# Splitting all 41 weight pieces of the second block on GpSimd during the last feed-forward stage

## The chip, the core and the metric

The kernel runs on one core of a Trainium2 chip. The metric is device time in microseconds (us) of one launch. The median of three runs of the kernel before is 1818.0 us (1817.51 to 1821.33). All array data is float32; one core computes the whole program.

## The reference

Two blocks work on x, 512 tokens of 1024 features. The first block has two layers; each adds a mixer, a cross-attention and a feed-forward part, with a layer norm after each. The second block modulates the normalised result by a condition vector, projects it, and runs two kinds of attention on it:

```python
def conv_ffn(x, w_up, conv_w, conv_b, w_down):
    up = x @ w_up
    a, g = up[..., :D_FF], up[..., D_FF:]
    g = causal_dwconv(g, conv_w) + conv_b
    return (jax.nn.gelu(g) * a) @ w_down
...
        mod = c_act @ w_ada[l] + b_ada[l]
        shift, scale, gate = jnp.split(mod, 3, axis=-1)
        h = rms_norm(x, norm_g[l]) * (1.0 + scale[:, None, :]) + shift[:, None, :]
        proj = h @ w_in[l]
...
        y = jnp.concatenate([y_r * jax.nn.silu(g_r), y_a * jax.nn.silu(g_a)], axis=-1)
        x = x + gate[:, None, :] * (y @ w_out[l])
```

## The kernel before, in words

**Matmuls.** Activations lie transposed: 8 tiles of 128 features x 512 tokens. A product is made to nearly full float32 precision out of three float32r matmuls (`mm3`, lines 304 to 306): each operand is kept as a rounded part (hi) and a remainder (lo), and hi*hi, hi*lo and lo*hi are summed in PSUM. A weight *piece* is 128 x 1024, so 24 matmuls of 512 columns use one piece. Its hi and lo together are 1 MB, its raw form 512 KB.

**How a piece gets into SBUF.** `piece` loads the raw 512 KB on the SP queue (line 241) into a raw buffer (two `raw`, one `rawx`), ScalarE casts hi (line 229) and VectorE subtracts to get lo (line 230), both into a `w` or `wx` tile (4 + 2 in the first block). In the second block (`extra` is 0) the subtraction is GpSimd's, there are only the 4 `w` tiles, and both come under the same lines 229 and 230.

**Splitting ahead.** In the second layer's feed-forward stage `ffn(1, ...)` GpSimd, otherwise nearly idle, prepares pieces of the second block: `pre_step` copies one element of a fresh result into the load buffer (line 264; this only makes the load wait for that result, which paces it), loads the raw piece on its own queue (line 265), casts and subtracts (lines 271 and 272), and stores the 1 MB result in DRAM (line 275). Load and result share one of two `vt` tiles. One load is issued per call, and the split of the piece before it. There are 22 calls after hidden tiles and 16 after the first two down-projection chunks, for 28 pieces. `ready` later loads the 1 MB straight into a `w` tile on SP (line 282); pieces that are not prepared go through `piece`. Not prepared are the five `OPEN` pieces with which the second block begins (`open2`) and the eight pieces of the output projection (`out_begin`, `out_end`).

**The stages that matter here.** (1) At the end of the first cross-attention, `lin` runs its last six output pieces in token halves, and `ln_half` normalises the first half while TensorE works on the second: sums by `res_stat` on GpSimd (lines 411 and 412), an averaging matmul (line 429), then VectorE and GpSimd (lines 435 to 442). In the same stretch the vector `mod` is begun: `ada_step` loads `w_ada` in 48 parts of 256 KB into `kt` tiles on SP (line 722) and accumulates them on VectorE (lines 726 and 728). They belong to the next stage, but the scheduler, which fixes every queue's order when the program is built and draws a ready instruction forward into what it takes for a gap, has put them here. (2) The last feed-forward stage, about 1043 to 1409 us. (3) The seam: the norm of each half, then `modulate` (ScalarE squares at line 449, averaging matmuls at line 757, VectorE and ScalarE at lines 765 to 767), while TensorE works on the other half and on the five `OPEN` pieces. (4) The second block, whose chains of small VectorE steps are interleaved with weight matmuls by a hand-written list with costs (`ORDER`, `FILL`). (5) The end: outputs are gated (lines 1161 to 1169), four output pieces are begun with six of eight input tiles each, then `out_end` finishes these and does the other four.

Of the kernel before, what the change touches and what calls it, by code (L numbers as in the profile page):

```python
# [8 lines left out]
F32 = mybir.dt.float32  # L9
F32R = mybir.dt.float32r  # L10
# [29 lines left out]
FILL = (1.12, 3, 1.5, 4, 2.08, 4.16, 23.8, 9, 4.2, 0.4, 4)  # L40
DVE_SUB = (0, 2, 5)
OPEN = (16, 0, 4, 8, 1)
STAG = 0
LASTD = 6
KS = (0, 1, 2, 3, 4, 5)
NPART = 4
# [13 lines left out]
def f32(ap):  # L60
    return ap.bitcast(F32)
# [73 lines left out]
def layout(i):  # L135
    i = {k: np.asarray(v) for k, v in i.items()}
    a = {}
    a["cst"] = constants()
    a["vec"] = pack_vecs(i)
    a["xT"] = np.ascontiguousarray(i["x"][0].T).reshape(KT, P, S)  # L140
    a["memT"] = np.ascontiguousarray(i["mem"][0].T.reshape(4, 2, P, MEM).transpose(0, 2, 1, 3))
    w = i["ab_w_in"][0]
    a["ab_u"] = stationary(w[:, :512])
    a["ab_v"] = moving(w[:, 512:1024])
    a["ab_x"] = stationary(w[:, 1024:])
    a["ab_o"] = stationary(i["ab_w_out"][0])
    a["sgu_row"] = np.ascontiguousarray(
        np.concatenate([i["sgu_ln_g"][0], i["sgu_ln_b"][0], i["sgu_b"][0].reshape(-1)])[None])
    a["sgu_wT"] = np.ascontiguousarray(i["sgu_w"][0].transpose(2, 0, 1))
    a["pool_w"] = np.ascontiguousarray(i["pool_w"][0].transpose(1, 0, 2).reshape(P, 512))  # L150
    a["c_in"] = stationary(i["c_w_in"][0])
    a["c_o"] = stationary(i["c_w_out"][0])
    for l in range(2):
        a[f"xq{l}"] = stationary(i["xa_wq"][l])
        a[f"xk{l}"] = stationary(i["xa_wkv"][l][:, :D])
        a[f"xv{l}"] = moving(i["xa_wkv"][l][:, D:])
        a[f"xo{l}"] = stationary(i["xa_wo"][l])
        a[f"up{l}"] = stationary(i["ffn_w_up"][l])
        for c, (f0, f1) in enumerate(CHUNKS):
            a[f"dn{l}{c}"] = stationary(i["ffn_w_down"][l], f0 * P, f1 * P)  # L160
    a["ada"] = np.ascontiguousarray(i["w_ada_2"][0].reshape(KT, P, 6, S).transpose(0, 2, 1, 3))
    w = i["w_in_2"][0]
    a["in_r"] = stationary(w[:, :2688 + 512])
    a["in_va"] = moving(w[:, 3200:3712])
    a["in_ga"] = stationary(w[:, 3712:])
    a["lora"] = np.ascontiguousarray(np.concatenate([i["w2_2"][0], i["a2_2"][0]]))
    idx = np.clip(np.arange(64)[:, None] - np.arange(S)[None] + 448, -63, 128) + 63
    a["rb"] = np.ascontiguousarray(i["rel_bias_2"][0][:, idx]).reshape(4, P, S)
    a["out"] = stationary(i["w_out_2"][0])
    return a  # L170


class Prog:
# [69 lines left out]


    def pre_begin(self):
        self.prep, todo = {}, []
        for _, ws in ORDER:
            for w in ws.split("+"):
                k, m = w[0], int(w[1:])
                if k in "rq" and m not in OPEN:  # L250
                    todo.append(("in_r", m))
                elif k == "g":
                    todo.append(("in_r", 12 + m) if m < 4 else ("in_ga", m - 4))
                elif w == "v0":
                    todo += [("in_va", i) for i in range(4)]
        self.todo, self.due2 = todo, []

    def pre_step(self, at):

        nc = self.nc  # L260
        if self.todo:
            key = self.todo.pop(0)
            t = self.t("vt", [P, 2, D], F32, 2)
            nc.gpsimd.tensor_copy(t[:, 1, 0:1], at[:, 0:1])
            nc.gpsimd.dma_start(out=t[:, 1, :], in_=self.a[key[0]][key[1]])
            self.due2.append((key, t))
        if len(self.due2) > 1 or not self.todo:
            for key, t in self.due2[:1]:
                self.due2.pop(0)
                hi, lo = t[:, 0, :].bitcast(F32R), t[:, 1, :].bitcast(F32R)  # L270
                nc.gpsimd.tensor_copy(hi, t[:, 1, :])
                nc.gpsimd.tensor_tensor(out=lo, in0=t[:, 1, :], in1=t[:, 0, :], op=ALU.subtract)
                name = f"sp_{key[0]}{key[1]}"
                d = self.prep[key] = self.dram.tile([P, 2, D], F32, tag=name, name=name)
                nc.gpsimd.dma_start(out=d, in_=t)

    def ready(self, src, m):

        if (src, m) not in self.prep:
            return self.piece(self.a[src][m])  # L280
        w = self.wtile()
        self.nc.sync.dma_start(out=f32(w), in_=self.prep[src, m])
        return w
# [139 lines left out]
    def ln_half(self, ts):  # L423
# [14 lines left out]
        for k in range(KT):  # L438
            x = self.x[k][:, ts]
            gk, bk = self.v(g, layer * 8 + k), self.v(b, layer * 8 + k)  # L440
            (nc.vector if k in DVE_SUB else nc.gpsimd).tensor_tensor(out=x, in0=x, in1=mn, op=ALU.subtract)  # L441
            nc.vector.scalar_tensor_tensor(out=x, in0=x, scalar=gk, in1=rs, op0=ALU.mult, op1=ALU.mult)  # L442
            if split:
                hi, lo = self.xs[k][:, 0, ts], self.xs[k][:, 1, ts]
                nc.scalar.activation(hi, x, AF.Identity, bias=bk)  # L445
                nc.vector.scalar_tensor_tensor(out=lo, in0=x, scalar=bk, in1=f32(hi), op0=ALU.add, op1=ALU.subtract)  # L446
            else:
                self.sqs.append(self.t("kt", [P, S], F32, 8))
                nc.scalar.activation(self.sqs[k][:, :256], x, AF.Square, bias=bk)
        if split:  # L450
            for k in range(KT):
# [114 lines left out]
    def kv(self, l, tag):  # L566
        nc = self.nc
        mem = []
        for j in range(4):
            raw = self.t("kt", [P, S], F32, 8)  # L570
            nc.sync.dma_start(out=raw.rearrange("p (a b) -> p a b", a=2), in_=self.a["memT"][j])
            t = self.xh() if tag == "xh" else self.hd()
            self.split(t, raw)
# [8 lines left out]
        kt, vt = [], []  # L582

        def epi_k(m, ps, ts):
            t = self.t("kt", [P, 2, MEM], F32R, 8)
            kt.append(self.split(t, ps[:, :MEM]))

        self.lin(f"xk{l}", range(8), mem, epi_k, MEM)
        vt = [self.t("vt", [P, 2, D], F32R, 2) for _ in range(2)]
# [70 lines left out]
    def ffn(self, l, xs):  # L660
# [3 lines left out]
        for c, (f0, f1) in enumerate(CHUNKS):  # L664
# [3 lines left out]
            def epi(m, ps, ts):  # L668
# [9 lines left out]
                else:  # L678
# [1 line left out]
                    nc.vector.tensor_tensor(out=h, in0=ps, in1=keep["g"], op=ALU.mult)  # L680
                    hs.append(self.split(self.hd(), h))
                    if l == 1:
                        self.pre_step(f32(hs[-1][:, 0, :]))

            self.lin(f"up{l}", [o + f for f in range(f0, f1) for o in (NF, 0)], xs, epi, first=FIRST if c == 0 else 0)

# [3 lines left out]
            def epi_d(m, ps, ts):  # L690
# [5 lines left out]
                if c == 1 and l == 0 and m == 1:  # L696
                    self.ada_end()
                if c < 2 and l == 1:
                    self.pre_step(x)
                if c == 2:  # L700
                    self.res_stat(m, ts)

# [13 lines left out]

    def ada_step(self, f):
        nc = self.nc
        while self.ada_at < min(48, 3 * (f + 1)):
            k, part = divmod(self.ada_at, 6)  # L720
            raw = self.t("kt", [P, S], F32, 8)
            nc.sync.dma_start(out=raw, in_=self.a["ada"][k, part])
            dst = self.acc[part // 4][:, part % 4 * S : part % 4 * S + S]
            sc = self.cact[:, k : k + 1]
            if k == 0:
                nc.vector.tensor_scalar(out=dst, in0=raw, scalar1=sc, scalar2=None, op0=ALU.mult)
# [43 lines left out]
    def open2(self):  # L770
# [1 line left out]
        self.nw = 3  # L772
        self.due = []
        for i, m in enumerate(OPEN):
            self.due.append((m, self.piece(self.a["in_r"][m]), self.bank()))
            self.half2(*self.due[-1], HALVES[0])
            if i == DEFER:
                self.flush()
# [319 lines left out]
    def rwkv_chain(self, prs, tt):  # L1098
# [77 lines left out]
        n = 0  # L1176
        while any(lines):
            for i, g in enumerate(lines):
                if g and n >= i * STAG:
                    us = next(g, None)  # L1180
                    if us is None:
                        lines[i] = None
# [247 lines left out]
```

## Time and profile before

| | us |
|---|---|
| median of 3 runs | 1818.0 |
| the profiled execution | 1816.8 |
| its span, first to last instruction | 1815.0 |
| TensorE busy | 1765.0 |
| VectorE busy | 1085.1 |
| ScalarE busy | 745.6 |
| GpSimd busy | 429.9 |
| mean granted TensorE clock | 0.989 of full |

The rows name engines by PE (TensorE), DVE (VectorE), ACT (ScalarE), POOL (GpSimd), SP (SyncE, which only issues transfers). Times in a timeline are us from the span's start. A row of a timeline ends, in brackets, with the idle time of the engine before it and what ended that. "x4" after a row means four instructions in one piece.

### The profile page before, as it was taken

To read this page: it belongs to the slowest core of one execution; us is meant where nothing else is said; L and a number is where in the kernel's file an instruction comes from. 1 tells how busy PE (TensorE), PEld (TensorE's weight loads), DVE (VectorE), ACT (ScalarE), POOL (GpSimd) and SP (SyncE) were. 2 spreads that over 40 slices of the span, in tenths; PEclk is the share of its full clock that TensorE was granted. 3 is DMA by queue.
4 is the path that set the end of the run, shared out by engine and by line. 5 is a ranking of instruction groups with operands and counts; after the bars stand their busy time and mean duration, and the time that the engine had idled before them with its cause. 6 is when DMAs were issued, how large, how long until landed. Compare 5 with 4: busy or idle time off the path is not lost.

```text
span 1815.0 us, 26295 instructions
## 1 busy us (share of the span) xinstructions
PE 1765.0 (97%) x10452; PEld 1489.2 (82%) x10452; DVE 1085.1 (60%) x1679; ACT 745.6 (41%) x1237; POOL 429.9 (24%) x438
## 2 busy tenths in 40 slices
PE   8999998999999999999999999999999989999999
PEld 7889988888888898988998998888888866776667
DVE  5676689743453458544476585365354875773672
ACT  5544533532332346322265453133233653434561
POOL 0215015000000042000320524464455232210122
PEclk9999999999999999999999999999999999998999
DMA  8431355332323224433131146677663444461332
GB/s 279 157 103 56 129 179 184 119 102 93 93 81 107 85 64 145 150 101 99 53 114 50 47 163 243 221 256 264 210 236 124 126 167 173 164 208 70 130 125 95
DMA packets 70555, 252.54 MB, mean 139 GB/s; under 512 B 8224, under 2 KB 10912, under 8 KB 62752
## 3 DMA queue, kind: packets, MB, share of 16 engines
q1 hardware_dynamic: 54288, 188.51, 31.6%
q0 software_dynamic: 11312, 53.48, 8.6%
q10 hardware_dynamic: 4832, 8.88, 1.5%
q8 instruction: 82, 1.34, 0.3%
q14 instruction: 41, 0.34, 0.1%
HBM read 212.30 MB, written 38.54 MB: 138 GB/s over the span
## 4 chain that ended last, share of the span: by engine, by line
PE 79%; DVE 12%; ACT 4%; DMA 3%; issue 2%; POOL 0%; SPq 0%; ACTq 0%; DVEq 0%; POOLq 0%
PE ch L304 10%; PE ch L305 10%; PE ch L306 10%; PE mm L304 9%; PE mm L306 9%; PE mm L305 9%; PE pv L305 3%; PE pv L304 3%; PE pv L306 3%; PE ch L881 3%; DVE w L230 1%; DVE x L442 1%; DVE xh L446 1%; DVE x L441 1%; PE at L1240 1%
## 5 line engine op out<-in xcount | busy, mean ns | idle before, releaser
L304 PE MATMUL mm<-xh,w 128*128 128x512 f32 (+1 forms) x696 | 260.7, 375 | 8.5 <-ACT w L229 5.6
L306 PE MATMUL mm<-xh,w 128*128 128x512 f32 (+1 forms) x696 | 254.9, 366 | 0.8 <-DVE w L230 0.8
L305 PE MATMUL mm<-xh,w 128*128 128x512 f32 (+1 forms) x696 | 253.9, 365 | 0.0
L411 POOL TENSOR_TENSOR t<-x,x 128x512 f32<-128x512 f32 x6 | 8.9, 1480 | 690.7 <-DVE x L420 354.9
L304 PEld LDWEIGHTS mm<-xh,w 128*128 128x128 f32 x696 | 132.9, 191 | 35.0 <-issue 9.2
L229 ACT CAST w<-raw 128x1024 fp32r<-128x1024 f32 (+2 forms) x98 | 98.7, 1008 | 139.9 <-PE ch L306 62.2
L304 PE MATMUL ch<-xh,w 128*128 128x512 f32 (+1 forms) x432 | 152.4, 353 | 1.9 <-ACT xh L445 1.9
L305 PE MATMUL ch<-xh,w 128*128 128x512 f32 (+1 forms) x432 | 153.1, 354 | 0.8 <-DVE xh L446 0.5
L306 PEld LDWEIGHTS mm<-xh,w 128*128 128x128 f32 x696 | 133.0, 191 | 24.1 <-issue 3.2
L306 PE MATMUL ch<-xh,w 128*128 128x512 f32 (+1 forms) x432 | 152.0, 352 | 0.7 <-DVE w L230 0.7
L305 PEld LDWEIGHTS mm<-xh,w 128*128 128x128 f32 x696 | 133.1, 191 | 23.8 <-issue 4.6
L229 ACT CAST wx<-raw 128x1024 fp32r<-128x1024 f32 (+1 forms) x85 | 88.1, 1039 | 154.0 <-PE ch L306 68.3
L230 DVE TENSOR_TENSOR w<-rawx,w 128x1024 fp32r<-128x1024 f32 (+2 forms) x85 | 106.0, 1247 | 69.7 <-ACT w L229 69.4
L230 DVE TENSOR_TENSOR w<-raw,w 128x1024 fp32r<-128x1024 f32 (+2 forms) x90 | 121.3, 1348 | 32.9 <-ACT w L229 32.5
L230 DVE TENSOR_TENSOR wx<-raw,wx 128x1024 fp32r<-128x1024 f32 (+1 forms) x85 | 120.4, 1418 | 29.0 <-ACT wx L229 28.6
L229 ACT CAST w<-rawx 128x1024 fp32r<-128x1024 f32 (+2 forms) x85 | 87.3, 1027 | 116.7 <-PE mm L306 69.7
L304 PE MATMUL ch<-xh,wx 128*128 128x512 f32 (+1 forms) x304 | 103.5, 341 | 0.0
L306 PE MATMUL ch<-xh,wx 128*128 128x512 f32 (+1 forms) x304 | 103.0, 339 | 0.0
L305 PE MATMUL ch<-xh,wx 128*128 128x512 f32 (+1 forms) x304 | 103.0, 339 | 0.0
L304 PE MATMUL mm<-hd,w 128*128 128x256 f32 (+1 forms) x304 | 98.0, 323 | 3.6 <-ACT hd L229 3.6
L306 PE MATMUL mm<-hd,w 128*128 128x256 f32 (+1 forms) x304 | 98.3, 323 | 0.0
L305 PE MATMUL mm<-hd,w 128*128 128x256 f32 (+1 forms) x304 | 97.7, 321 | 0.0
(495 smaller groups left out, 4498.7 us busy)
## 6 DMA issues: line engine op xcount, KB each, us to landing
raw<-in_up SPq DMA_DIRECT2D x56, 512.0 KB, 3.6
sp_in_r<-vt POOLq DMA_DIRECT2D x20, 1024.0 KB, 5.2
w<-sp_in_r SPq DMA_DIRECT2D x20, 1024.0 KB, 5.1
rawx<-in_up SPq DMA_DIRECT2D x32, 512.0 KB, 3.5
kt<-in_ada SPq DMA_DIRECT2D x48, 256.0 KB, 3.7
raw<-in_dn SPq DMA_DIRECT2D x24, 512.0 KB, 3.5
vt<-in_in_r POOLq DMA_DIRECT2D x20, 512.0 KB, 6.5
raw<-in_c_in SPq DMA_DIRECT2D x16, 512.0 KB, 3.5
```

The costliest lines, as they stand in the source:

```text
L229: nc.scalar.copy(hi, src)
L230: (eng or nc.vector).tensor_tensor(out=lo, in0=src, in1=f32(hi), op=ALU.subtract)
L304: mm(out, lhsT=ah, rhs=bh, start=start, stop=False)
L305: mm(out, lhsT=ah, rhs=bl, start=False, stop=False)
L306: mm(out, lhsT=al, rhs=bh, start=False, stop=stop)
L411: eng.tensor_tensor(out=sz, in0=self.x[0][:, ts] if m == 1 else sz, in1=z, op=ALU.add)
L441: (nc.vector if k in DVE_SUB else nc.gpsimd).tensor_tensor(out=x, in0=x, in1=mn, op=ALU.subtract)
L442: nc.vector.scalar_tensor_tensor(out=x, in0=x, scalar=gk, in1=rs, op0=ALU.mult, op1=ALU.mult)
L446: nc.vector.scalar_tensor_tensor(out=lo, in0=x, scalar=bk, in1=f32(hi), op0=ALU.add, op1=ALU.subtract)
L881: self.tc.keep_in_program_order(self.nc.tensor.matmul(out, **kw))
L1240: nc.tensor.matmul(ps[hs, :w], lhsT=q[hs, c * 64 : c * 64 + 64], rhs=k[hs, :w], start=True, stop=True)
```

## The change

All 41 pieces of the second block (the five `OPEN` and eight output pieces too) are split by GpSimd in `ffn(1, ...)`. A raw piece goes into a `kt` tile of its own (4 tiles of 4 KB per partition instead of 8 of 2 KB), only the result into a `vt` tile. A split comes in the code when two later loads are issued (`PRE_LAG`). The number of loads follows a count of work done: 2 for a hidden tile, 1 for an output tile of the first two chunks, out of 60, with the last load 4 before the end. `piece` is no longer used in the second block. As `kt` tiles are now 4 KB, `w_ada` comes in 24 parts of 512 KB, one `kt` tile holds two of the eight key tiles of the cross-attention, and the two halves of a `kt` tile serve two feature tiles in the last norm. A constant that had no effect (`STAG`) goes.

```diff
-    a["ada"] = np.ascontiguousarray(i["w_ada_2"][0].reshape(KT, P, 6, S).transpose(0, 2, 1, 3))
+    a["ada"] = np.ascontiguousarray(i["w_ada_2"][0].reshape(KT, P, 3, D).transpose(0, 2, 1, 3))
...
-        self.prep, todo = {}, []
+        self.prep, todo = {}, [("in_r", m) for m in OPEN]
...
+                elif k == "o":
+                    todo += [("out", i) for i in range(8)]
         self.todo, self.due2 = todo, []
-
-    def pre_step(self, at):
-
-        nc = self.nc
-        if self.todo:
-            key = self.todo.pop(0)
-            t = self.t("vt", [P, 2, D], F32, 2)
-            nc.gpsimd.tensor_copy(t[:, 1, 0:1], at[:, 0:1])
-            nc.gpsimd.dma_start(out=t[:, 1, :], in_=self.a[key[0]][key[1]])
-            self.due2.append((key, t))
-        if len(self.due2) > 1 or not self.todo:
...
+        self.pre_n, self.pre_at, self.pre_all = len(todo), 0, 2 * NF + 2 * KT
+
+    def pre_step(self, at, part):
+
+        self.pre_at += part
+        left = self.pre_n - -(-self.pre_n * self.pre_at // (self.pre_all - 4))
+        while self.todo and len(self.todo) > left:
+            while len(self.due2) > PRE_LAG:
+                self.pre_split()
+            self.pre_load(at)
+        while self.due2 and not self.todo:
+            self.pre_split()
+
+    def pre_load(self, at):
+        nc = self.nc
+        key = self.todo.pop(0)
+        raw = self.t("kt", [P, D], F32, 4)
+        nc.gpsimd.tensor_copy(raw[:, 0:1], at[:, 0:1])
+        nc.gpsimd.dma_start(out=raw, in_=self.a[key[0]][key[1]])
+        self.due2.append((key, raw))
+
+    def pre_split(self):
+        nc = self.nc
+        key, raw = self.due2.pop(0)
+        t = self.t("vt", [P, 2, D], F32, 2)
+        nc.gpsimd.tensor_copy(t[:, 0, :].bitcast(F32R), raw)
+        nc.gpsimd.tensor_tensor(out=t[:, 1, :].bitcast(F32R), in0=raw, in1=t[:, 0, :], op=ALU.subtract)
+        name = f"sp_{key[0]}{key[1]}"
+        d = self.prep[key] = self.dram.tile([P, 2, D], F32, tag=name, name=name)
+        nc.gpsimd.dma_start(out=d, in_=t)
...
-        if (src, m) not in self.prep:
-            return self.piece(self.a[src][m])
         w = self.wtile()
         self.nc.sync.dma_start(out=f32(w), in_=self.prep[src, m])
...
-                self.sqs.append(self.t("kt", [P, S], F32, 8))
+                if k % 2 == 0:
+                    two = self.t("kt", [P, D], F32, 4)
+                    self.sqs += [two[:, :S], two[:, S:]]
...
-                        self.pre_step(f32(hs[-1][:, 0, :]))
+                        self.pre_step(f32(hs[-1][:, 0, :]), 2)
...
-                    self.pre_step(x)
+                    self.pre_step(x, 1)
...
-        while self.ada_at < min(48, 3 * (f + 1)):
-            k, part = divmod(self.ada_at, 6)
-            raw = self.t("kt", [P, S], F32, 8)
+        while self.ada_at < min(24, 2 * (f + 1)):
+            k, part = divmod(self.ada_at, 3)
+            raw = self.t("kt", [P, D], F32, 4)
...
-            self.due.append((m, self.piece(self.a["in_r"][m]), self.bank()))
+            self.due.append((m, self.ready("in_r", m), self.bank()))
```

## Rows read from the trace of the kernel before

**Rows 1.** The page, busy time of each engine, its share of the span, instructions

```profile
PE 1765.0 (97%) x10452; PEld 1489.2 (82%) x10452; DVE 1085.1 (60%) x1679; ACT 745.6 (41%) x1237; POOL 429.9 (24%) x438
```

**Rows 2.** Waits of TensorE over the span: total us, times, longest

```profile
PE at L429 <- POOL t L411: 5.8, 3, 4.9
...
PE at L757 <- ACT kt L449: 5.4, 2, 2.7
...
PE pv L1263 <- DVE rt L1272: 2.0, 1, 2.0
```

**Rows 3.** Four stretches: us, busy of PE, PEld, DVE, ACT, POOL; PEclk, DMA share, GB/s

```profile
1180.00:1260.00 80.00, 80.00 (x354) 66.25 (x353) 50.66 (x45) 29.21 (x38) 46.42 (x43) 1.00 0.74 261
...
284.00:291.00 7.00, 6.55 (x23) 5.54 (x23) 5.55 (x10) 1.50 (x4) 1.12 (x2) 0.52 0.87 277
...
1407.00:1410.40 3.40, 3.40 (x9) 2.70 (x10) 3.40 (x7) 3.40 (x10) 0.98 (x1) 0.52 0.30 123
...
1760.00:1766.00 6.00, 5.21 (x24) 3.71 (x24) 6.00 (x9) 2.77 (x4) 2.75 (x2) 0.72 0.42 134
```

**Rows 4.** VectorE's groups, 236 to 300 us, its timeline there, and the chain there

```profile
L728 DVE SCALAR_TENSOR_TENSOR vt<-kt,cact,vt 128x512 f32<-128x512 f32 x36 | 31.8, 932 | 0.0
...
271.26 3.69 DVE L728 SCALAR_TENSOR_TENSOR vt<-kt,cact,vt 128x512 f32<-128x512 f32 x4
...
277.11 2.94 DMA kt<-in_ada
```

**Rows 5.** VectorE's timeline at the seam: start, us, instruction

```profile
1403.01 0.62 DVE L391 TENSOR_TENSOR rstd<-rstd,t 128x256 f32<-128x256 f32 x1
1403.56 1.75 DVE L230 TENSOR_TENSOR w<-raw,w 128x1024 fp32r<-128x1024 f32 x1
1405.23 3.71 DVE L442 SCALAR_TENSOR_TENSOR x<-x,vec,rstd 128x256 f32<-128x256 f32 x8
...
1424.69 1.21 DVE L230 TENSOR_TENSOR w<-raw,w 128x1024 fp32r<-128x1024 f32 x1
1425.83 0.41 DVE L435 TENSOR_TENSOR t<-at,t 128x256 f32<-128x256 f32 x1
```

**Rows 6.** The instructions on tile vt: duration in ns min/median/max, first and last start

```profile
L271 POOL CAST vt<-vt x28: 1033/1047/2130, 1076.2 to 1370.2; 128x1024 fp32r<-128x1024 f32 x28
L272 POOL TENSOR_TENSOR vt<-vt x28: 2378/2404/3326, 1077.3 to 1371.3; 128x1024 fp32r<-128x1024 f32 x28
```

**Rows 7.** GpSimd's timeline in the last feed-forward stage

```profile
1119.67 1.05 POOL L271 CAST vt<-vt 128x1024 fp32r<-128x1024 f32 x1 [6.30 <-DMA vt<-in_in_va]
...
1197.06 0.53 POOL L265 DMA_DIRECT2D vt<-in_in_r  x1 [0.30 <-POOL vt L264]
1198.78 2.09 POOL L271 CAST vt<-vt 128x1024 fp32r<-128x1024 f32 x1 [1.19 <-DMA vt<-in_in_r]
...
1382.33 2.05 POOL L411 TENSOR_TENSOR t<-x,x 128x512 f32<-128x512 f32 x1 [7.77 <-ACT w L229]
```

**Rows 8.** Transfers by kind: count, KB each, median us to landing

```profile
w<-sp_in_r SPq DMA_DIRECT2D x20, 1024.0 KB, 5.1
...
w<-sp_in_ga SPq DMA_DIRECT2D x4, 1024.0 KB, 6.5
```

**Rows 9.** VectorE's timeline near the end of the second block

```profile
1748.83 2.48 DVE L230 TENSOR_TENSOR ar<-y,ar 128x512 fp32r<-128x512 f32 x1 [1.03 <-ACT ar L229]
...
1756.92 0.68 DVE L230 TENSOR_TENSOR ar<-y,ar 128x512 fp32r<-128x512 f32 x1
1757.52 2.62 DVE L390 TENSOR_SCALAR bh<-bh 128x512 f32<-128x512 f32 x1
```

**Rows 10.** GpSimd's timeline near the end

```profile
1748.37 2.39 POOL L230 TENSOR_TENSOR w<-raw,w 128x1024 fp32r<-128x1024 f32 x1 [2.44 <-ACT w L229]
...
1757.50 2.36 POOL L230 TENSOR_TENSOR w<-raw,w 128x1024 fp32r<-128x1024 f32 x1 [2.95 <-ACT w L229]
...
1786.24 4.77 POOL L230 TENSOR_TENSOR w<-raw,w 128x1024 fp32r<-128x1024 f32 x2 [20.04 <-ACT w L229]
```

More of the change, by code (lines that the diff above doesn't have):

```diff
@@ L42 @@
 OPEN = (16, 0, 4, 8, 1)
-STAG = 0
+PRE_LAG = 2
 LASTD = 6
@@ L255, in pre_begin @@
                     todo += [("in_va", i) for i in range(4)]
+                elif k == "o":
+                    todo += [("out", i) for i in range(8)]
         self.todo, self.due2 = todo, []
-    def pre_step(self, at):
-        nc = self.nc
-        if self.todo:
-            key = self.todo.pop(0)
-            t = self.t("vt", [P, 2, D], F32, 2)
-            nc.gpsimd.tensor_copy(t[:, 1, 0:1], at[:, 0:1])
-            nc.gpsimd.dma_start(out=t[:, 1, :], in_=self.a[key[0]][key[1]])
-            self.due2.append((key, t))
-        if len(self.due2) > 1 or not self.todo:
[L268 to L275, printed above, removed]
+        self.pre_n, self.pre_at, self.pre_all = len(todo), 0, 2 * NF + 2 * KT
@@ L569, in kv @@
         for j in range(4):
-            raw = self.t("kt", [P, S], F32, 8)
+            raw = self.t("kt", [P, D], F32, 4)[:, :S]
             nc.sync.dma_start(out=raw.rearrange("p (a b) -> p a b", a=2), in_=self.a["memT"][j])
@@ L584, in epi_k @@
         def epi_k(m, ps, ts):
-            t = self.t("kt", [P, 2, MEM], F32R, 8)
-            kt.append(self.split(t, ps[:, :MEM]))
+            if m % 2 == 0:
+                self.two = self.t("kt", [P, 4, MEM], F32R, 4)
+            kt.append(self.split(self.two[:, m % 2 * 2 : m % 2 * 2 + 2], ps[:, :MEM]))
         self.lin(f"xk{l}", range(8), mem, epi_k, MEM)
@@ L718, in ada_step @@
         nc = self.nc
-        while self.ada_at < min(48, 3 * (f + 1)):
-            k, part = divmod(self.ada_at, 6)
-            raw = self.t("kt", [P, S], F32, 8)
+        while self.ada_at < min(24, 2 * (f + 1)):
+            k, part = divmod(self.ada_at, 3)
+            raw = self.t("kt", [P, D], F32, 4)
             nc.sync.dma_start(out=raw, in_=self.a["ada"][k, part])
-            dst = self.acc[part // 4][:, part % 4 * S : part % 4 * S + S]
+            dst = self.acc[part // 2][:, part % 2 * D : part % 2 * D + D]
             sc = self.cact[:, k : k + 1]
@@ L1178, in rwkv_chain @@
             for i, g in enumerate(lines):
-                if g and n >= i * STAG:
+                if g:
                     us = next(g, None)
```

## The prediction

> **What bounds the kernel.** I read the busy times first: TensorE is busy for 1765 of 1815 us [rows 1], so no other engine's relief counts except where TensorE stands. The waits of TensorE say where that is. Of those that the change can touch, three are long: 4.9 us at the averaging matmul of the first cross-attention's norm, behind GpSimd's sum, 5.4 us in two pieces at the averaging matmuls of `modulate`, behind ScalarE's squares, and 2.0 us near the end, behind a VectorE copy [rows 2]. The stretches then show a second price of such a wait. In 284 to 291 us, right after the first of them, the granted clock is 0.52, which is mostly the 1.2 GHz level; so it is in 1407 to 1410.4, after the first wait in `modulate`, and it is 0.72 in 1760 to 1766, after the wait near the end [rows 3]. What is missing to full clock is lost in each: 7 x 0.48 = 3.4 us, 3.4 x 0.48 = 1.6 us and 6 x 0.28 = 1.7 us. In 80 us of the last feed-forward stage, on the other hand, TensorE is busy for 80.00 us at full clock, while the transfer engines are at 0.74 and GpSimd at 46 of 80 us [rows 3]. There is nothing to gain there, only cover to lose.
>
> **Term 1, `w_ada` in 24 parts for 48.** The sum that TensorE waited for comes out of residual adds on VectorE, and between them VectorE has the accumulation: 36 instructions for 31.8 us, 0.93 us each on 512 elements [rows 4]. A part of 1024 elements lies between 1.21 us (VectorE's two-input instruction of that length [rows 5]) and 2 x 0.93 = 1.86 us. Four old ones stand between two adds, 3.69 us [rows 4]; two new ones take 2.4 to 3.7 us. Over the six adds of the half that is 0 to 7.8 us, and it can give back at most the wait of 4.9 and the 3.4 us of clock, 8.3 us. But the same 12.6 MB must come, and the chain shows VectorE waiting 2.94 us for one part [rows 4]; with four tiles for eight such a wait can also grow by its own length. Bounds: +8.3 and -2.9 us. I take a gain of 3.0, about halfway, since the bytes don't shrink.
>
> **Term 2, thirteen more splits in the feed-forward stage.** One split on GpSimd takes 1.05 + 2.40 us [rows 6], the issues of its load and store 0.53 us each [rows 7], the small copy and gaps, by my estimate, about 1 us: some 5.5 us. 41 of them are 226 us, and from the first cast at 1076.2 [rows 6] to the residual sums at 1382.3, where GpSimd is next needed [rows 7], there are 306. It fits if casts don't wait. The transfers grow by 13 x 1.5 MB over some 300 us, 68 GB/s, on top of 261 [rows 3]; the shares scale to about 0.93. Raw weights for TensorE come one per 24 matmuls, which is 24 x 80/354 = 5.4 us [rows 3], into three buffers, so a transfer that takes twice its time is still covered. VectorE is busy for 51 of 80 us there [rows 3] and gets slower beside GpSimd; the cover is the rest of its time. If it goes, each late piece costs TensorE what it is late by. I take a loss of 0.5 us, bounds 0 and 3. The queue moved past is GpSimd's own: behind the splits stand only the sums at 1382 us (a rival, below). The waits that are new, a cast for its load and for the store of two pieces earlier, hold up nothing else.
>
> **Term 3, the seam.** Five casts and five subtractions of `OPEN` pieces go from ScalarE and VectorE. One subtraction stands on the chain that TensorE waits for: it runs from 1403.56 for 1.75 us, and the scaling that feeds the squares, ready at 1403.63, starts at 1405.23 [rows 5]: 1.6 us. In the second half, one subtraction delays the variance by about 0.3 us [rows 5]. If the first wait falls from 2.7 to 1.1 us, I expect the clock not to fall: 1.6 us [rows 3]. That is 3.5 us. The other three subtractions lie in gaps of VectorE, so they give nothing. What is new: each piece, 1 MB, can start only when its `w` tile is free and lands 5.1 us later [rows 8], where a preloaded piece needed only its subtraction, 1.2 us [rows 5], and a cast, taken as long as GpSimd's, 1.05 us [rows 6]. The tiles come free one by one as the six last output pieces finish, and the norm's chain stands between that and the first use; this hides it. Bounds: 7 us gained (both waits of 2.7 and the clock) and, if the cover goes, 8 us lost (a rival).
>
> **Term 4, the second block and its end.** 28 pieces are loaded as before. Near the end GpSimd's subtractions of output pieces go. Two VectorE instructions there take 2.48 and 2.62 us; the first of these forms takes 0.68 us a little later [rows 9]. Beside each of the two a subtraction of 2.4 us starts at the same time on GpSimd [rows 10]. Both are in the chain before the copy that TensorE waits 2.0 us for. So I take the 2.0 back, and 1.0 of the 1.7 us of clock: 3.0 us, bounds 0 and 3.7. The Trainium skill, in "SBUF — State Buffer", section "SBUF: two separate sides", says that GpSimd and VectorE contend for one port pair, and that the loser waits for the whole instruction; the 2.4 us of a subtraction and the 1.8 us of added time agree. By that rule the 13 added subtractions would also each hold VectorE for up to 2.4 us in the feed-forward stage, 31 us in all, which would be no gain but a loss if VectorE were the bound there; the rows say that it is not. Against the gain: in `out_end` the fifth piece's `w` tile comes free with the first finished product. Before, ScalarE cast the piece then, and GpSimd began to subtract at 1786.24 and was done with the first of two by 1788.6 [rows 10]; a cast of 1.05 us and its start put the free tile at about 1785. Now the load needs 5.1 to 6.5 us [rows 8], 1790.1 to 1791.5 us. TensorE has three more products to finish, 18 matmuls of 0.226 us or 4.1 us, so it would stand 1.0 to 2.4 us. I take 1.3. `STAG` is nothing; the key tiles and the memory loads in pairs only share tiles that were free anyway; if that cover fails, it is a wait of one ScalarE or VectorE step, under 1 us.
>
> **The sum.** -3.0 + 0.5 - 3.5 - 3.0 + 1.3 = -7.7 us, on the profiled execution's 1816.8: 1809.1. That execution lies 1.2 us under the median of 1818.0, so for a median I say 1810. The scheduler makes the order of each queue anew from the first changed part on, which moves small waits in the second block; I allow 4 us either way, and the forecast's own range is 1801 to 1814.
>
> **Rivals.**
> *GpSimd falls behind (slower).* "Two behind its load" is the order in the code; the queue's order is the scheduler's. The trace shows casts drawn forward to right behind their own load: one waits 6.30 us for it, while another, further on, waits 1.19 [rows 7]. Before, the 28 casts start 294/27 = 10.9 us apart [rows 6], and nobody minded. 41 have room for 306/41 = 7.5 us each; beyond that every microsecond counts 41 times, because the sums of the last norm stand behind them on GpSimd and TensorE waits. At 8.2 us that is 29 us late, about 1840; at the 10.9 of before it is 139 us, about 1950. Against it: loads no longer need the tile of a store, and with half again as many pieces there are fewer gaps to draw a cast into; a piece needs 5.5. 12 in 100. It is also the case in which the change doesn't do what it says.
> *Late loads at the seam (slower).* SP's queue is in order. If the load for a late tile stands early in it, the others stand behind it: that tile is free only when the output piece behind `modulate`'s first matmuls is done, after 1410.4 [rows 3], say 1412, and four more loads of 5.1 us each [rows 8] are there by 1433. The last subtraction but one ended at 1425.9 [rows 5], so that is some 8 us late: with terms 1, 2 and 4 at -4.2, 1818.0 - 4.2 + 8 = 1822. 7 in 100.
> *The gains are eaten (no change).* Removed waits were not the last ones: the residual adds wait for the same bytes, the second half's chain at the seam takes up what the first gave. Then term 4 remains and some of the rest, 1815 to 1820, about 1817. 15 in 100.
> *The norm's wait of the first layer goes entirely (faster still).* 8.3 us for 3.0, and both waits in `modulate` with the clock, 7.0 for 3.5: 1810 - 5.3 - 3.5 = 1801, down to 1797. 10 in 100.
>
> **The numbers.** The forecast itself has 56 in 100. A measurement of this kernel can tell about 0.2%, 3.6 us: faster is under 1814.4, slower over 1821.6. Faster: 0.56 + 0.10 = 0.66. Same: 0.15 and 0.01 of the late loads, 0.16. Slower: 0.12 + 0.06 = 0.18. The range for 8 in 10 goes from 1797 (the fourth rival) to 1826 (late loads with some spread) and leaves out GpSimd's falling behind and little more.
>
> **What would show it.** In the profile after: the wait at line 429 near 283 us shorter than 4.9 us; no subtraction at line 230 between lines 391 and 442 at the seam, and a wait at line 757 near 1 us with full clock behind it; no VectorE instruction of 2.5 us near the end; a wait of TensorE of about 1 us at the fifth output piece, released by a load; GpSimd's last store of a split before 1382 us. I'd be wrong if a wait for GpSimd's sums stands before the last norm, if TensorE waits for `w` loads at the seam, or if new waits in 1460 to 1740 us outweigh the gains.

## The result, and the profile after

The changed kernel takes **1847.62 us** (median of 4 runs, 1844.08 to 1856.4), the kernel before 1817.76 us in the same series (4 runs): ratio 1.0167, 95% interval [1.0145, 1.0189]. It is slower by 29.9 us, where the prediction said 1810 and 1797 to 1826. The profiled execution took 1849.04 us with a span of 1847.3.

Lines of the code have moved: the norm's averaging matmul is L440 now (429 before), GpSimd's sums L422 and L423 (411, 412), the squares of the last norm L462 (449), the averaging matmul of `modulate` L771 (757), the split's cast and subtraction L284 and L285, its load and store L277 and L288.

The page of the changed kernel: busy times, the granted clock in 40 slices, and the chain that ended last by engine.

```profile
PE 1766.4 (96%) x10452; PEld 1489.9 (81%) x10452; DVE 1083.1 (59%) x1650; ACT 734.1 (40%) x1224; POOL 478.4 (26%) x495
...
PEclk9999999999999999999999999999995999998999
...
PE 62%; DMA 12%; DVE 10%; POOL 8%; issue 5%; ACT 3%; SPq 0%; POOLq 0%; ACTq 0%; DVEq 0%
```

TensorE does the same work in about the same busy time as before [rows 1] and the span is 32.3 us longer, so it stands that much longer. The waits of TensorE over the span (total us, times, longest) say where:

```profile
PE at L440 <- POOL t L422: 37.3, 3, 34.1
...
PE at L771 <- ACT kt L462: 4.7, 3, 2.6
...
PE mm L315 <- DMA w<-sp_out: 2.0, 1, 2.0
```

One wait of 34.1 us for GpSimd's sums is more than the whole loss. The other two rows answer to [rows 2]: the waits at `modulate` have hardly shrunk (5.4 before), the 2.0 us behind a VectorE copy are gone, and a wait of 2.0 us for the fifth output piece is new. What GpSimd does before those sums, its timeline at the end of the last feed-forward stage (start, us, instruction, in brackets the idle time before it and who ended it):

```profile
1403.95 0.53 POOL L277 DMA_DIRECT2D kt<-in_out  x1 [0.30 <-POOL kt L276]
1409.86 1.04 POOL L284 CAST vt<-kt 128x1024 fp32r<-128x1024 f32 x1 [5.38 <-DMA kt<-in_out]
1410.98 2.33 POOL L285 TENSOR_TENSOR vt<-kt,vt 128x1024 fp32r<-128x1024 f32 x1
1413.62 0.57 POOL L288 DMA_DIRECT2D sp_out<-vt  x1 [0.30 <-POOL vt L285]
1414.21 1.27 POOL L422 TENSOR_TENSOR t<-x,x 128x512 f32<-128x512 f32 x1
```

The sums started at 1382.33 before [rows 7] and start at 1414.21 now, right behind the last split. That last cast stands directly behind its own load and waits 5.38 us for it; in the code the splits of the two pieces before it stand between them. Two stretches of the changed kernel (us, then busy time of PE, PEld, DVE, ACT, POOL, the granted clock, the share of the transfer engines, GB/s) show that nothing else in the stage went wrong:

```profile
1100.00:1360.00 260.00, 260.00 (x1138) 213.15 (x1137) 146.77 (x128) 77.28 (x95) 161.25 (x155) 1.00 0.79 280
...
1391.00:1428.00 37.00, 5.14 (x16) 4.43 (x17) 0.42 (x1) 2.49 (x7) 19.86 (x24) 0.50 0.34 128
```

In the feed-forward stage TensorE is busy for all of 260 us at full clock, as in the stretch of [rows 3]. In the second stretch, which is mostly the wait, GpSimd itself is busy for only half of the time. It is not short of speed; it waits for transfers.

### The profile page after: what moved, and what is told of

Same layout as the page of the kernel before. It is cut to its first block, busy times and chain, and to the rows that moved or that the text cites. A ratio compares the mean times of both kernels' runs of the same rounds, so it can differ in the third digit from the quotient of the medians.

```text
span 1847.3 us, 26266 instructions
## 1 busy us (share of the span) xinstructions
PE 1766.4 (96%) x10452; PEld 1489.9 (81%) x10452; DVE 1083.1 (59%) x1650; ACT 734.1 (40%) x1224; POOL 478.4 (26%) x495
## 4 chain that ended last, share of the span: by engine, by line
PE 62%; DMA 12%; DVE 10%; POOL 8%; issue 5%; ACT 3%; SPq 0%; POOLq 0%; ACTq 0%; DVEq 0%
PE mm L315 8%; PE mm L317 8%; PE mm L316 8%; PE ch L315 7%; PE ch L316 7%; PE ch L317 7%; DMA kt<-in_in_r 4%; POOL vt L285 3%; DMA sp_in_r<-vt 3%; PE ch L895 3%; PE pv L316 3%; PE pv L315 3%; PE pv L317 3%; POOL vt L284 2%; DMA kt<-in_out 2%
## 5 line engine op out<-in xcount | busy, mean ns | idle before, releaser
L422 POOL TENSOR_TENSOR t<-x,x 128x512 f32<-128x512 f32 x6 | 8.8, 1461 | 683.5 <-ACT w L229 328.0
L315 PEld LDWEIGHTS mm<-xh,w 128*128 128x128 f32 x696 | 134.5, 193 | 35.5 <-issue 9.1
L316 PEld LDWEIGHTS mm<-xh,w 128*128 128x128 f32 x696 | 134.7, 194 | 23.9 <-issue 4.6
L317 PEld LDWEIGHTS mm<-xh,w 128*128 128x128 f32 x696 | 134.4, 193 | 24.1 <-issue 3.2
L230 DVE TENSOR_TENSOR w<-rawx,w 128x1024 fp32r<-128x1024 f32 (+2 forms) x84 | 112.5, 1340 | 67.0 <-ACT w L229 66.5
L229 ACT CAST w<-raw 128x1024 fp32r<-128x1024 f32 (+2 forms) x88 | 88.3, 1004 | 129.1 <-PE ch L317 62.8
L285 POOL TENSOR_TENSOR vt<-kt,vt 128x1024 fp32r<-128x1024 f32 x41 | 105.3, 2569 | 1.8
L315 PE MATMUL mm<-hd,w 128*128 128x256 f32 (+1 forms) x304 | 98.5, 325 | 3.6 <-ACT hd L229 3.6
L317 PE MATMUL mm<-hd,w 128*128 128x256 f32 (+1 forms) x304 | 98.7, 325 | 0.0
```

Source lines behind the costliest of these rows:

```text
L229: nc.scalar.copy(hi, src)
L230: (eng or nc.vector).tensor_tensor(out=lo, in0=src, in1=f32(hi), op=ALU.subtract)
L285: nc.gpsimd.tensor_tensor(out=t[:, 1, :].bitcast(F32R), in0=raw, in1=t[:, 0, :], op=ALU.subtract)
L315: mm(out, lhsT=ah, rhs=bh, start=start, stop=False)
L316: mm(out, lhsT=ah, rhs=bl, start=False, stop=False)
L317: mm(out, lhsT=al, rhs=bh, start=False, stop=stop)
```

## The experiments

Five questions: is it the order of GpSimd's queue; does the number of pieces matter; how near to its load may a cast stand; what is each of the other parts worth; and what does the end cost. Ratios are against the kernel before, run in the same series.

| kernel | us, median (runs) | ratio [95%] | TensorE's wait before the last norm, us |
|---|---|---|---|
| changed | 1847.62 (4) | 1.0167 [1.0145, 1.0189] | 34.1 |
| e1_pinned: casts kept in the order of the code | 1814.39 (11) | 0.9976 [0.9965, 0.9988] | none |
| e2_ada_only: `w_ada` in 24 parts and shared tiles alone | 1814.60 (11) | 0.9971 [0.9958, 0.9985] | none |
| e4_pinned_no_open: pinned, 36 pieces | 1814.96 (12) | 0.998 [0.9963, 0.9998] | none |
| e5_pinned_no_out: pinned, 33 pieces | 1815.96 (12) | 0.998 [0.9967, 0.9992] | none |
| e6_pinned_out4: pinned, 37 pieces | 1814.21 (10) | 0.9965 [0.9951, 0.998] | none |
| e7_loose_39: free order, 39 pieces | 1856.14 (4) | 1.02 [1.0176, 1.0224] | 37.4 |
| e8_loose_36: free order, 36 pieces | 1855.06 (4) | 1.0192 [1.0168, 1.0217] | 39.1 |
| e9_own_load: pinned right behind the own load | 1868.17 (3) | 1.0271 [1.0246, 1.0296] | 47.7 |
| e10_one_behind: pinned, one behind | 1815.47 (10) | 0.999 [0.9976, 1.0004] | none |
| e11_out4_again: e6 once more | 1812.71 (12) | 0.9972 [0.996, 0.9984] | none |
| e12_pinned_again: e1 once more | 1816.35 (12) | 0.9994 [0.9981, 1.0006] | none |

### Is it the order? (e1_pinned)

The changed kernel with one thing more: the scheduler may not move the cast of a split out of the order in which the code gives it.

```diff
-        nc.gpsimd.tensor_copy(t[:, 0, :].bitcast(F32R), raw)
+        self.tc.keep_in_program_order(nc.gpsimd.tensor_copy(t[:, 0, :].bitcast(F32R), raw))
```

> Edit: the changed kernel with one thing more: each cast of a split is tied, in GpSimd's queue, behind what stands before it in the code, so behind the load two pieces later. Nothing else of the work changes. Theory A (the order of the queue: casts drawn forward wait for their own loads, about 100 us of waits on 41 pieces, and GpSimd comes 34 us late to the sums of the last norm): the waits of the casts for loads fall under 25 us, the last store of a split comes before 1375 us, TensorE's 34.1 us at line 440 shrink to under 1 us, and with them the half-clock stretch of 37.5 us; time 1806 to 1815. Theory B (the rate: 41 pieces with 1.5 MB of transfers each and the shared SBUF port take about 8.5 us each however they are ordered): the casts still start about 8.4 us apart, now waiting for stores or running longer; time 1838 to 1850.

Measured: 1814.39 us, and the 34-us wait is gone. GpSimd's waits from 1060 to 1415 us in the changed kernel, the five longest (total us, times, longest):

```profile
POOL vt L284 <- DMA kt<-in_in_r: 63.7, 11, 8.4
POOL vt L284 <- DMA kt<-in_out: 32.3, 6, 6.4
POOL vt L284 <- DMA sp_in_r<-vt: 20.4, 8, 4.9
POOL kt L276 <- ACT hd L229: 15.0, 1, 15.0
POOL vt L284 <- DMA sp_in_va<-vt: 4.1, 3, 1.7
```

and of the pinned kernel in the same stretch, its longest and those of a split's cast for a transfer of an `in_r` or an output piece:

```profile
POOL kt L276 <- ACT hd L229: 64.9, 12, 15.0
...
POOL vt L284 <- DMA sp_in_r<-vt: 2.1, 4, 1.1
...
POOL vt L284 <- DMA kt<-in_in_r: 1.1, 1, 1.1
...
POOL vt L284 <- DMA sp_out<-vt: 0.5, 1, 0.5
```

The casts' waits for their own loads fall from 101.7 us (63.7 + 32.3, and 3.3 and 2.4 for the other two kinds) to 1.1. The order of GpSimd's instructions in the traces says the same: in the changed kernel 21 of the 41 casts have no other cast between their load and themselves, and these 21 have all the waits for own loads; in the pinned kernel 39 have two, as in the code. What is left is the small copy before a load that waits for the feed-forward's activations (ACT hd): now the pacing sets the rhythm, as the code meant. The 41 casts run from 1072.6 to 1359.3 us, 7.2 us apart, and the last starts 23 us before the sums of [rows 7]. So the cause is the order of GpSimd's queue; the instructions, the bytes and the tiles are the same in both kernels.

### Does the number of pieces matter? (e7_loose_39, e8_loose_36)

The free order again, with fewer pieces. In e7 the last two output pieces, in e8 the five of `OPEN` are loaded raw and split in the second block; `ready` falls back to `piece` for them.

```diff
-                    todo += [("out", i) for i in range(8)]
+                    todo += [("out", i) for i in range(6)]       # e7
-        self.prep, todo = {}, [("in_r", m) for m in OPEN]
+        self.prep, todo = {}, []                                 # e8
```

> The changed kernel with its casts free to be moved forward, as it is, but 39 pieces in place of 41 (the last two output pieces are loaded raw). Theory A (each piece takes GpSimd 8.46 us because casts wait for their own loads, and only what does not fit before the last norm is late): two pieces fewer are 17 us less, TensorE's wait before the last norm falls from 34 to about 17 us, the time to about 1830 (1826 to 1834). Theory B (the wait comes from the free order itself or from the tiles shared in the last stage, whatever the count): a wait of 30 us or more stays, and the time is over 1840.

> The changed kernel with its casts free to be moved forward, but 36 pieces (the five of the opening list are loaded raw and split at the seam as before). Theory A (8.46 us per piece): five pieces fewer are 42 us less, more than the 34 us by which the changed kernel was late, so the last norm waits for nothing: 1814 to 1818, the same as with pinned casts. Theory B (the free order costs whatever the count): over 1835.

Measured: 1856.14 and 1855.06 us, waits of 37.4 and 39.1 us. My theory A of these runs, a fixed price of 8.46 us for each piece, fell: five pieces fewer, and the wait is 5 us longer. The 36-piece kernel's tile `vt` (ns min/median/max, first and last start), and GpSimd's waits from 1060 to 1425 us:

```profile
L284 POOL CAST vt<-kt x36: 1032/1044/2035, 1073.4 to 1418.5; 128x1024 fp32r<-128x1024 f32 x36
```

```profile
POOL vt L284 <- DMA kt<-in_in_r: 81.7, 15, 7.2
POOL vt L284 <- DMA kt<-in_out: 38.9, 7, 6.6
POOL vt L284 <- DMA kt<-in_in_ga: 19.8, 3, 6.9
```

36 casts take 345 us, 9.9 us each, against 8.46 in the changed kernel: with fewer pieces more of them stand right behind their own load (with the 6.4 us in 2 for `in_va`, 27 of 36, against 19 of 41). That direction agrees with the sentence of the prediction that more pieces leave fewer gaps to draw a cast into; what it got wrong is that half the casts were still drawn. The same count over all kernels, from the same two views, from the first cast to the last norm:

| kernel | pieces | casts that wait for their own load: number, us | first and last cast | us apart | late by |
|---|---|---|---|---|---|
| before | 28 | 22, 106.1 | 1076.2, 1370.2 | 10.9 | 0 |
| e8 | 36 | 27, 146.8 | 1073.4, 1418.5 | 9.9 | 39.1 |
| e7 | 39 | 26, 130.3 | 1071.9, 1414.9 | 9.0 | 37.4 |
| changed | 41 | 19, 101.7 | 1071.5, 1409.9 | 8.5 | 34.1 |
| e9 | 41 | 30, 140.4 | 1075.4, 1429.6 | 8.9 | 47.7 |
| e10 | 41 | 13, 18.1 | 1075.3, 1356.4 | 7.0 | 0 |
| e1 | 41 | 1, 1.1 | 1072.6, 1359.3 | 7.2 | 0 |

One sum fits all of them within 2 in 100 where GpSimd did not wait for its pacing: some 5.4 us of GpSimd for a piece (cast 1.05, subtraction 2.40, the two issues 1.1, a copy and two gaps 0.8), plus what its casts wait. For 36 pieces 194 + 147, and 7 for stores, is 348 us; from the first cast to the end of the last split it was some 349 us. For 41 it is 221 + 102 + 24 = 347, measured 342. Why the scheduler draws 27 casts of 36 forward and 19 of 41 is not shown by these runs.

### How near may the cast stand? (e9_own_load, e10_one_behind)

The pinned kernel with another distance in the code: `PRE_LAG` 0 and 1 for 2.

```diff
-PRE_LAG = 2
+PRE_LAG = 0      # e9; 1 in e10
```

> All 41 pieces, the casts kept in the order of the code, but that order put right behind each piece's own load (lag 0 for 2). Theory A (what is late is late because GpSimd stands for the load in front of it: a stretch of such pieces in the 36-piece run has them 12.2 to 12.8 us apart): 40 x 12.2 = 488 us from the first cast at 1072, so the last at about 1560 and the last norm some 180 us late: 1980 to 2000 us. Theory B (the lateness of the loose kernels comes from the freedom of the order as such, and a fixed order overlaps the next load): under 1880.

> All 41 pieces, the casts kept in the order of the code, one behind their loads (lag 1 for 2). Theory A: between a load's issue and its cast lie the split of the piece before (1.05 + 2.40 + 0.3 + 0.57 us), a copy and the next load (some 1.0 us), 5.4 us of the 6.1 to 7.3 that it takes to land; the cast waits 0.7 to 1.9 us, a piece takes 6.1 to 7.3 us, under the 7.5 that there are, and nothing is late: 1813 to 1818. Theory B (a second piece of distance is needed, because landings stretch when loads and stores of two pieces overlap): each piece over 8 us, 1835 or more.

Measured for e9: 1868.17 us. Theory A's number fell: a piece does not take 12.2 us. Theory B's number, under 1880, held, and so did its second half, that a fixed order overlaps the next load; its first half did not. The lateness comes with a fixed order too when that order puts the cast behind its own load (47.7 us, the longest of all), so it is the place of the cast and not the freedom as such. GpSimd's timeline of e9 shows why:

```profile
1106.33 1.04 POOL L284 CAST vt<-kt 128x1024 fp32r<-128x1024 f32 x1 [3.23 <-DMA sp_in_r<-vt]
...
1109.82 0.58 POOL L277 DMA_DIRECT2D kt<-in_in_r  x1
1110.39 0.53 POOL L288 DMA_DIRECT2D sp_in_r<-vt  x1
1114.78 1.04 POOL L284 CAST vt<-kt 128x1024 fp32r<-128x1024 f32 x1 [3.85 <-DMA kt<-in_in_r]
```

Only the cast was held; the next load was moved ahead of the store, so part of its landing was covered, and these two casts are 8.45 us apart. A variant with the loads held too was not tried.

Measured for e10: 1815.47 us, nothing late, casts 7.0 us apart, and 18.1 us of waits for own loads in 13 casts, 1.4 us each. So one piece of other work between a load and its cast is enough, as theory A had it: 5.4 us of GpSimd's work against a landing of 5.4 us (median of the 25 `in_r` pieces in e10; 6.1 in e1, 7.3 in the changed kernel).

### What are the other parts worth? (e2_ada_only, e4_pinned_no_open, e5_pinned_no_out)

e2 is the kernel before with only the part on `w_ada` (24 parts, tiles of `kt` in fours, two keys and two squares to a tile); e4 and e5 are the pinned kernel without the opening pieces and without the output pieces.

```diff
-        while self.ada_at < min(48, 3 * (f + 1)):                # e2, on the kernel before
-            k, part = divmod(self.ada_at, 6)
+        while self.ada_at < min(24, 2 * (f + 1)):
+            k, part = divmod(self.ada_at, 3)
...
-        self.prep, todo = {}, [("in_r", m) for m in OPEN]        # e4, on the pinned one
+        self.prep, todo = {}, []
...
-                elif k == "o":                                   # e5, on the pinned one
-                    todo += [("out", i) for i in range(8)]
```

> Edit: the kernel before with only the kt tiles of 4 KB and the 24 parts of w_ada, with the key tiles and the last norm's squares in pairs; the splitting ahead stays as it was, 28 pieces. Theory A (fewer, longer accumulations on VectorE leave the residual adds of the first cross-attention less late): the last feed-forward stage begins some 5 us earlier than before, as it did in the changed kernel, and all of that reaches the end: 1811 to 1814. Theory B (what the first stage gains is only another order of waits, and comes back later): 1816 to 1820.

> Edit: the pinned kernel, but the five OPEN pieces are not prepared and go through load, cast and VectorE subtraction at the seam, as before; 36 pieces are split ahead. It prices term 3 (the seam) against the pinned kernel. Theory A (one subtraction on the norm's chain and the clock that falls after the longer wait): 2 to 5 us slower than the pinned kernel. Theory B (the chain of the second half takes up what the first gives): within 1.5 us of it.

> Edit: the pinned kernel, but the eight output pieces are not prepared: they are loaded raw, cast on ScalarE and subtracted on GpSimd in the second block, as before; 33 pieces are split ahead. It prices term 4 (the end). Theory A (as predicted, 3 us gained on VectorE's chain against 1.3 us of wait for the fifth output piece): 1 to 3 us slower than the pinned kernel. Theory B (the load that replaces cast and subtraction costs its wait of 2 us and a fall of the clock behind it, and the relief of VectorE gives nothing): 1 to 4 us faster than the pinned kernel.

Measured: the part on `w_ada` alone is 4.3 us under the kernel before (1818.89 us in that series) and as fast as all parts together with pinned casts. At 1814.60 us it lies between the ranges of its two theories. Leaving out the opening pieces or the output pieces changes nothing that can be measured: the three pinned medians lie within 1.6 us and their intervals overlap. So beside `w_ada` the two terms at the seam and the end come to about nothing; the next pair says of the end why.

### What does the end cost? (e6_pinned_out4, e11_out4_again, e12_pinned_again)

The pinned kernel with the first four output pieces prepared and the last four loaded raw, so that the fifth is loaded ahead of the end again; then once more beside the fully prepared one.

```diff
-                    todo += [("out", i) for i in range(8)]
+                    todo += [("out", i) for i in range(4)]
```

> The pinned casts of the first experiment, with only the first four of the eight output pieces prepared (37 pieces in all); the last four are loaded raw and split as in the kernel before, so that the fifth one is loaded ahead of the end again. Theory A (the relief of VectorE near the end is real, about 3 us, and is given back at the fifth output piece, where the load is 2.1 us late and the clock halves behind it): that wait goes, the relief stays, and the time is 3 to 4 us under the fully prepared kernel: about 1811, ratio 0.995 to 0.996. Theory B (the end's gain and loss were both the scheduler's scatter; the raw pieces' subtractions on GpSimd hold VectorE up again): 1814 to 1816, ratio 0.997 to 0.998.

> The pinned kernel with only the first four output pieces prepared, once more, beside the fully prepared one in the same call. If the late load of the fifth output piece costs what one profile showed (a 2.1 us wait and half clock behind it): 2 to 4 us under the fully prepared one. If not: within 1 us of it.

> The pinned kernel with all 41 pieces, once more: 1814 to 1816, a wait of about 2 us at the fifth output piece, and half clock behind it.

Measured: e6 alone left it open (ratio 0.9965, its median 1814.21). Side by side, e11 takes 1812.71 us and e12 1816.35: 3.6 us, in the 2 to 4 expected. The intervals of the two ratios touch ([0.996, 0.9984] and [0.9981, 1.0006]); the 12 times of each, held against each other without the kernel before, have means 4.3 us apart, with a 95% interval from 1.9 to 6.7. The traces have the same sum. VectorE's additions to the fourth and the fifth finished output piece, in e12 (the code of e11 stands two lines further on):

```profile
1779.09 0.75 DVE L1353 SCALAR_TENSOR_TENSOR mk<-ch,mod,mk 128x512 f32<-128x512 f32 x1 [0.61 <-PE ch L317]
1788.40 0.75 DVE L1353 SCALAR_TENSOR_TENSOR mk<-mm,mod,mk 128x512 f32<-128x512 f32 x1 [8.56 <-PE mm L317]
```

and in e11:

```profile
1779.04 0.75 DVE L1355 SCALAR_TENSOR_TENSOR mk<-ch,mod,mk 128x512 f32<-128x512 f32 x1 [0.61 <-PE ch L319]
1784.57 0.75 DVE L1355 SCALAR_TENSOR_TENSOR mk<-mm,mod,mk 128x512 f32<-128x512 f32 x1 [4.78 <-PE mm L319]
```

9.3 us against 5.5. In e12 TensorE's timeline begins with the late load and goes on at half speed:

```profile
1781.01 0.47 PE L315 MATMUL mm<-ar,w 128*128 128x512 f32 x1 [1.96 <-DMA w<-sp_out]
1781.32 0.39 PE L316 MATMUL mm<-ar,w 128*128 128x512 f32 x1
...
1782.40 0.63 PE L317 MATMUL mm<-ar,w 128*128 128x512 f32 x1
...
1784.96 0.62 PE L317 MATMUL mm<-ar,w 128*128 128x512 f32 x1
1785.39 0.44 PE L315 MATMUL mm<-xh,w 128*128 128x512 f32 x1
```

The matmuls come 0.23 us apart until 1782, 0.43 until 1785.4, and 0.23 again. The granted clock is 1.00, 0.51 and 0.98 in these three stretches. So the late load costs 1.96 us of standing and 1.7 of clock (3.4 us at 0.51), 3.6 of the 3.8 us between the two kernels. e6 and e11 are faster than the kernel before and than the changed one, by 0.3% and by 1.9 to 2.0% of its time; against e2, which changes far less, they can't be told apart.

## Why the prediction was wrong

**The step that failed** is in term 2: "41 of them are 226 us, and ... there are 306. It fits if casts don't wait", at a price of 0.5 us with bounds 0 and 3, and with it the sentence that gave the rival 12 in 100: "with half again as many pieces there are fewer gaps to draw a cast into; a piece needs 5.5". Casts did wait, 19 of 41, 101.7 us in all, and the rival named as "GpSimd falls behind" is what happened, by its mechanism and nearly at its price: it said 29 us late and about 1840 at 8.2 us for a piece; the trace shows 8.46 us, 34.1 us late, 1847.6.

The rows that I rested this on were two single casts, one with 6.30 us of wait and one with 1.19 [rows 7]. The view that would have priced it is the list of GpSimd's own waits, which I did not use. Of the kernel before, from 1060 to 1415 us:

```profile
POOL vt L271 <- DMA vt<-in_in_r: 69.6, 15, 7.8
POOL vt L264 <- DMA sp_in_r<-vt: 28.9, 10, 5.8
POOL vt L271 <- DMA vt<-in_in_va: 27.4, 4, 8.4
...
POOL vt L271 <- DMA vt<-in_in_ga: 9.1, 3, 5.6
```

22 of the 28 casts wait for their own load, 106.1 us; in the order of the queue the same number have no other cast in between. With some 31 us of waits for stores and 28 x 5.4 = 151 us of work that is 288 of the 294 us between the first and the last cast: before, GpSimd was not pacing itself at 10.9 us a piece, it was full. Carried over to 41 pieces at the same share, 41 x 5.4 + 41 x 22/28 x 4.8 = 376 us, it would have been 70 us late; with no waits, not late at all. Between these bounds a loss was the likelier side, and 12 in 100 was far too little.

**Term 2 otherwise held.** With the casts pinned, TensorE is busy for all of 260 us, with 0.85 of the transfer engines for 0.93 predicted and VectorE busy for 127.16 us against 133.34 before (in the changed kernel, with its loose order, it was 146.77; why it differs was not followed). The two stretches, first of e12, then of the kernel before:

```profile
1100.00:1360.00 260.00, 260.00 (x1138) 213.18 (x1137) 127.16 (x128) 77.65 (x95) 183.68 (x174) 1.00 0.85 308
```

```profile
1100.00:1360.00 260.00, 260.00 (x1137) 213.17 (x1137) 133.34 (x126) 76.85 (x94) 125.46 (x119) 1.00 0.68 237
```

The splits themselves cost nothing; the 0.5 was within its bounds.

**Term 1** was right in its size: 3.0 us predicted, 4.3 measured in e2 (its interval in the ratio, 0.9958 to 0.9985, is 2.7 to 7.6 us). In e2's profile the averaging matmul of the norm's second half, the first thing behind the accumulation, starts at 310.1 us, before at 313.2: 3.1 us. The single wait of 4.9 us [rows 2] became two, 3.1 and 1.5, the second of them behind that matmul; it was mostly split, not removed. Over the whole norm, from TensorE's 1500th matmul (254.13 us before, 254.82 in e2) to its 2000th (332.73 and 329.31), the gain is 4.1 us, and TensorE's waits there fall from 7.9 to 5.3 us. The clock gave nothing: from 276 to 296 us it is 0.83 in both, so the 8.3 us of this term's upper bound had 3.4 in them that did not move in e2 (in the changed kernel and e12, with the pieces prepared too, it is 0.91). At 1039.7 us, ahead of the last feed-forward stage, the lead is 4.8 us, but the 10000th matmul starts only 1.9 us earlier than before (1714.58 and 1712.70). The seam takes 2.9 back, and there the waits are the same two of 2.7 us. What differs is the clock; the kernel before, then e2:

```profile
1396.00:1440.00 44.00, 38.16 (x261) 35.20 (x260) 36.81 (x67) 30.03 (x66) 18.09 (x20) 0.96 0.36 116
```

```profile
1391.00:1435.00 44.00, 38.15 (x237) 34.38 (x236) 34.45 (x60) 27.40 (x59) 18.12 (x20) 0.88 0.33 105
```

44 us at 0.96 lose 1.8 us, at 0.88 5.3 us. With one profile of each kernel it stays open whether this is scatter or comes from the shared tiles at the seam.

**Term 3** predicted 3.5 us and is worth about nothing. The subtraction did leave the chain: in e12 the first matmul comes 2.1 us after the last step of the variance (1397.91 and 1399.97), before 3.8 us (1403.01 [rows 5] and 1406.77 below). But TensorE waits as long as before. The last matmul ahead of the averaging and the first of it, e12 and the kernel before:

```profile
1397.06 0.28 PE L317 MATMUL pv<-hd,wx 128*128 128x256 f32 x1
1399.97 5.28 PE L771 MATMUL at<-kt,cst 128*128 128x256 f32 x16 [2.64 <-ACT kt L462]
```

```profile
1403.81 0.28 PE L305 MATMUL ch<-hd,wx 128*128 128x256 f32 x1
1406.77 5.41 PE L757 MATMUL at<-kt,cst 128*128 128x256 f32 x16 [2.68 <-ACT kt L449]
```

The matmuls on `ch` that stood ahead of it stand behind it now. The scheduler, with a shorter chain to plan for, put the averaging one product earlier, and the wait is 2.64 for 2.68 us. This is read from the traces; holding TensorE's order there was not tried. The clock fell as well, which I had expected not to happen: 44 us of the seam are at 0.96 in e12 and e1, as before, and at 0.88 in e4, which splits the opening pieces there. So one profile can't price this term; the times can, and e4's median is 0.6 us over e1's. The rival of late loads at the seam did not come: TensorE waits for no `w` load there in the changed kernel or in e12.

**Term 4** had the mechanism right twice and one size wrong. The gain was predicted at 3.0: from the last matmuls of the recurrence's chain to the first output piece's addition it is 1756.67 to 1785.07 before, 28.4 us, and 1749.80 to 1775.01 in e12, 25.2: 3.2 us. VectorE's groups near the end, before (1740 to 1760 us) and in e12 (1733 to 1753 us): the one-input instruction and the subtraction that ran beside GpSimd's splits.

```profile
L390 DVE TENSOR_SCALAR bh<-bh 128x512 f32<-128x512 f32 x3 | 3.5, 1157 | 0.1
L230 DVE TENSOR_TENSOR ar<-y,ar 128x512 fp32r<-128x512 f32 x2 | 3.2, 1580 | 1.0 <-ACT ar L229 1.0
```

```profile
L230 DVE TENSOR_TENSOR ar<-y,ar 128x512 fp32r<-128x512 f32 x2 | 1.4, 690 | 0.1
...
L401 DVE TENSOR_SCALAR bh<-bh 128x512 f32<-128x512 f32 x3 | 1.3, 425 | 0.0
```

1580 ns fall to 690 and 1157 to 425 once no subtraction of GpSimd runs there. The Trainium skill, "SBUF — State Buffer", section "SBUF: two separate sides", has the loser of the port that GpSimd and VectorE share wait for the whole instruction; these rows agree. Its other consequence, up to 31 us more on VectorE in the feed-forward stage, did not come with pinned casts (127.16 for 133.34 us). The loss was predicted at 1.3 us, for a wait of 1.0 to 2.4: the wait is 2.0, but the clock behind it, 1.7 us, was not in the sum, although the same effect stood in [rows 3] for other waits. With 3.8 us the late load gives all of the gain back.

**The sum** with what was measured: from 1817.8, -4.3 for `w_ada`, nothing for the seam, +0.6 for the end and +34.1 for the sums is 1848.2; the changed kernel took 1847.6. That it closes so well is in part luck: the terms come from different series and single profiles, each good to a few us, and the half clock behind the long wait is not in it. Without the 34.1 it would be 1814, which is where the pinned kernels are (1814.4 and 1816.4).

## What to carry to other kernels

A distance between a load and its user that stands only in the program's order is worth what the scheduler leaves of it: look in the trace of before at how many instructions of the kind already stand right behind their own load, and price a larger number of them with the waits of that engine's queue, not with its busy time. If the distance matters, hold it in order; here one instruction held was worth 33 us, and one piece of other work between load and user was enough. And a short wait of TensorE is to be priced with the half clock behind it: here 2.0 us of standing had 1.7 us of lost clock behind them. That price is not fixed: at the seam the same two waits went with 1.8 us of lost clock in one kernel and 5.3 in another.

## What the runs showed of the hardware

The clock fell after a wait of 1.96 us, and not at once: in e12 the first matmuls behind it came at full pace for about 1.0 us (granted clock 1.00 from 1781 to 1782 us), and then 3.4 us were at half (0.51). In the changed kernel's long wait the granted clock is 0.50 from 1391 to 1428 us, that is, for some 5 us after TensorE went on at 1422.9.

A load of 512 KB landed later from GpSimd's queue than from SP's in the last feed-forward stage of the changed kernel. Its transfers from 1060 to 1415 us (queue, count, KB each, median us from issue to landing):

```profile
kt<-in_in_r POOLq DMA_DIRECT2D x25, 512.0 KB, 7.3
raw<-in_up SPq DMA_DIRECT2D x22, 512.0 KB, 4.4
...
raw<-in_dn SPq DMA_DIRECT2D x12, 512.0 KB, 5.8
```

In e1 the three are 6.1, 4.9 and 5.1 us and in e10 5.4, 4.9 and 5.9, so most of the gap goes with the loose order; that the queue as such is slower is not shown. I had the landing of raw pieces on that queue in no term; it is what each cast drawn forward waits for.
